# Softmax mixture on one core: VectorE makes the weights, and two stores are cut differently

## The chip, the cores and the metric

The kernel runs on one core of a Trainium2 chip. The metric is the device time of one execution in microseconds, as the median of the runs; lower is better. Five engines matter here: TensorE (PE, matmuls), VectorE (DVE), ScalarE (ACT), GpSimd (POOL) and SyncE (SP), which only issues transfers. Sixteen DMA engines move the data between HBM and the on-chip memory SBUF; TensorE writes its sums to PSUM. Each engine works through its own instructions in the order in which the program lists them, and waits on semaphores for the others.

## The reference

Four softmaxes over 4096 columns are mixed with weights that are themselves a softmax over the four heads:

```python
# logits: (32, 128, 4, 4096), prior: (32, 128, 4), float32
prior_probs = np.exp(prior - prior.max(axis=-1, keepdims=True))
prior_probs = prior_probs / prior_probs.sum(axis=-1, keepdims=True)
softmax = np.exp(logits - logits.max(axis=-1, keepdims=True))
softmax = softmax / softmax.sum(axis=-1, keepdims=True)
mixture = np.sum(prior_probs[..., None] * softmax, axis=2)   # (32, 128, 4096)
```

The input is 268 MB and the output 67 MB, and each is moved once.

## The kernel before

A unit is one of the 32 batches: 128 rows on the 128 partitions, four heads of 4096 columns. The tile `ring` has 12 slots of one head each, so three units lie in SBUF at a time. A head is worked on in place: it is loaded into its slot, its exponentials overwrite it, and the unit's result overwrites the slot of head 3 (`home`), from where it is stored.

The whole program is a list of words that `run` turns into instructions. A word is a letter for the step, the digits of its arguments (head, then first and last quarter of the columns), a prime for "the unit before", `+2` for "two units on" and `@u` for unit u. The steps are:

- `L` loads heads, `S` stores quarters of a unit (stores of units 2 to 21 are issued by ACT, all else by SP).
- `M` (VectorE) takes a row's negated maximum over 4096 columns, `E` (ACT) the exponentials with their row sum in `dsum`.
- `R` (VectorE) takes the reciprocal of that sum into `rden`. The weight of a head is this reciprocal times the prior probability `pp`.
- `G` (GpSimd) makes a 128x128 diagonal matrix of the weight: identity times `rden` times `pp`. `X` (TensorE) multiplies that diagonal with the exponentials and adds the heads up in PSUM (`acc`).
- `Z` (GpSimd) scales columns of a head by both numbers in place. `C` (GpSimd) multiplies both numbers into `wght`, which `K` (ACT, scaling) and `A`, `B`, `T` (VectorE, multiply by the weight and add) read.
- `O`, `P` and `W` (GpSimd) add columns of two slots, `V` (ACT) copies PSUM to SBUF.

So in a steady unit half of the columns go through TensorE for heads 0 to 2 and end with `A` on VectorE, and the other half are scaled by ACT (`K`) and GpSimd (`Z`) and added by GpSimd (`O`). The order of all this is written out by hand: `ORDER` has one line each for units 0 and 1, the line `STEADY` 22 times, and a long list for units 24 to 31 in which the steps of neighbouring units are interleaved. `BYPASS` names column quarters of which head 2 doesn't go through TensorE. Loads wait until the slots that they fill are free: for heads 0 to 2 until the last `O` of the old unit, for head 3 until its store has landed.

`store` cuts unit 28 (`U - 4`) into three transfers: the columns but the last 320 of all 128 rows, the last 320 of 125 rows, and the last 320 of the other 3 rows. Unit 31 is stored in halves, `S24` and `S02`.

Of the kernel before, what the change touches and what calls it, by code (L numbers as in the profile page):

```python
# [8 lines left out]
FP32 = mybir.dt.float32  # L9
AF = mybir.ActivationFunctionType  # L10
ALU = mybir.AluOpType
# [14 lines left out]

FIRST = "L02 L24"
STEADY = (
    "M0 E0 O224' R3' C3' Z324' M1 R0 G0 C0 O324' A01' A12' E1 S' L03+2 L34+2 K024 X002 "
    "M2 E2 R1 G1 X102 Z124 M3 E3 R2 G2 X202 C2 O124 K224 "  # L30
)

ORDER = [
# [3 lines left out]
] + [STEADY] * 22  # L37
ORDER += [
# [27 lines left out]
]  # L66

EXTRA = 320

BYPASS = {  # L70
    (27, 3), (28, 2), (28, 3), (29, 3), (30, 3), (31, 2), (31, 3),
# [4 lines left out]
def kernel(  # L76
# [6 lines left out]
    nc = tc.nc  # L83
    U, P, H, V = logits.shape
# [5 lines left out]
    C = V // 4  # L90

    cpool = ctx.enter_context(tc.tile_pool(name="cpool", bufs=1))
# [4 lines left out]

    nmax = cpool.tile([P, U, H], FP32, name="nmax")
    dsum = cpool.tile([P, U, H], FP32, name="dsum")
    rden = cpool.tile([P, U, H], FP32, name="rden")  # L100
    wght = cpool.tile([P, U, H], FP32, name="wght")
    diag = cpool.tile([P, 2, H - 1, P], FP32, name="diag")
    ident = cpool.tile([P, P], FP32, name="ident")
# [3 lines left out]
    pp = cpool.tile([P, H, U], FP32, name="pp")  # L107
# [4 lines left out]
    def slot(u, h, a=0, b=4):  # L112
        return ring[:, place(u, h), a * C : b * C]

    def home(u, a, b):
        return slot(u, 3, a, b)
# [8 lines left out]

    def store(u, a=0, b=4):
        queue = nc.scalar if 2 <= u < 22 else nc.sync
        if u == U - 4:

            o, c = home(u, a, b), V - EXTRA  # L130
            for p, q, i, j in ((0, P, 0, c), (0, 125, c, V), (125, P, c, V)):
                queue.dma_start(out=out[u, p:q, i:j], in_=o[p:q, i:j])
            return
        queue.dma_start(out=out[u, :, a * C : b * C], in_=home(u, a, b))

    def peak(u, h):
# [7 lines left out]
            accum_out=dsum[:, u, h : h + 1],  # L144
        )

    def recip(u, h):
        nc.vector.reciprocal(rden[:, u, h : h + 1], dsum[:, u, h : h + 1])  # L148

    def diagonal(u, h):  # L150
        nc.gpsimd.tensor_scalar(  # L151
            out=diag[:, u % 2, h], in0=ident, scalar1=rden[:, u, h : h + 1],
            scalar2=pp[:, h, u : u + 1], op0=ALU.mult, op1=ALU.mult,
        )


    def weigh(u, h, a=0, b=4):
        e = slot(u, h)
# [4 lines left out]
                start=h == 0, stop=h == H - 2 or (u, k * W // C) in BYPASS and h == H - 3,  # L163
            )

    def weight(u, h):
        nc.gpsimd.tensor_mul(wght[:, u, h : h + 1], rden[:, u, h : h + 1], pp[:, h, u : u + 1])  # L167

    def scale(u, h, a, b):
        e = slot(u, h, a, b)  # L170
        nc.gpsimd.tensor_scalar(  # L171
            out=e, in0=e, scalar1=rden[:, u, h : h + 1], scalar2=pp[:, h, u : u + 1],
            op0=ALU.mult, op1=ALU.mult,
        )

    def scale_act(u, h, a, b):
        e = slot(u, h, a, b)
# [28 lines left out]
    def add_scaled(u, a, b):  # L206
        nc.gpsimd.tensor_add(home(u, a, b), slot(u, 1, a, b), slot(u, 3, a, b))  # L207

    step = {
        "L": load, "S": store, "M": peak, "E": exp, "R": recip, "G": diagonal, "X": weigh,  # L210
        "C": weight, "Z": scale, "A": add_last, "B": add_head, "T": add_both, "V": evac,
        "P": add_scaled, "W": add_second,
        "K": scale_act, "O": add_below,
    }
# [10 lines left out]
    with tc.manual_schedule():  # L225
# [6 lines left out]
            out=ident, in_=ident, pattern=[[-1, P]], compare_op=ALU.is_equal, fill=0.0,  # L232
# [48 lines left out]
```

## Time and profile before

| | before |
|---|---|
| runs | 788.8, 786.51, 786.8 us; median 786.8 us |
| the profiled execution | 786.83 us, span 785.1 us |
| mean granted TensorE clock | 0.841 |
| busy: VectorE, ACT, GpSimd, TensorE | 82%, 75%, 73%, 60% of the span |
| moved by DMA | 335.83 MB, mean 428 GB/s |
| VectorE: 128 maxima of 4096 columns (line 137) | 563.0 us, 4409 ns each |
| ACT: 128 exponentials of 4096 columns (line 142) | 474.1 us, 3704 ns each |
| GpSimd: 68 additions of 2048 columns (line 182) | 308.5 us, 4537 ns each |
| GpSimd: 50 scalings of 2048 columns (line 171) | 102.4 us, 2047 ns each |
| GpSimd: 96 diagonals (line 151) | 43.0 us, 448 ns each |
| GpSimd: 79 weights of 128x1 (line 167) | 15.0 us, 189 ns each |
| VectorE: 128 reciprocals of 128x1 (line 148) | 19.4 us, 155 ns each |

The span runs from the first to the last instruction of the profiled execution; the time of the same execution is a little longer. Busy time is what an engine spent in instructions that compute. Times in the text are microseconds from the start of the span.

### The profile page before, as it was taken

The page shows a single profiled execution, that of the slowest core. Times are in us where ns is not written, and L with a number is a line of the kernel's source. Part 1 is how long each engine was busy: PE and PEld are TensorE (multiplying, and loading weights), DVE is VectorE, ACT ScalarE, POOL GpSimd, SP SyncE. Part 2 cuts the span into 40 slices and gives each one's busy share as a digit, 9 for nine tenths or more (in the row PEclk, how much of TensorE's full clock was granted, in tenths as well). Part 3 has the DMA queues.
Part 4 walks back from the last instruction along what each step waited for, and adds up shares of the span by engine and source line. Part 5 has one row for each costly group of instructions (what it writes and reads, how often), then busy time and mean ns, then how long its engine had stood idle before and what let it go on. Part 6 is the DMA issues. An engine that isn't in the chain of part 4 may idle for free.

```text
span 785.1 us, 3589 instructions
## 1 busy us (share of the span) xinstructions
PE 472.1 (60%) x920; PEld 189.7 (24%) x920; DVE 646.3 (82%) x326; ACT 590.1 (75%) x324; POOL 575.1 (73%) x342
## 2 busy tenths in 40 slices
PE   0445556554466444664446655456643988899996
PEld 0112212211122111221112222112211433334342
DVE  5589988797777977779877789777898877989895
ACT  1658887777878778787787877777878567779883
POOL 0799877788777788777887778877786434377892
PEclk9968898886887778887778777788777999999999
DMA  9999999999999999999999999999999999999997
GB/s 379 452 454 390 449 417 422 431 449 421 452 410 432 441 439 429 432 420 436 449 419 444 414 434 432 450 414 431 433 445 434 430 413 431 441 420 430 429 428 336
DMA packets 14747, 335.83 MB, mean 428 GB/s; under 512 B 1640, under 2 KB 1768, under 8 KB 1800
## 3 DMA queue, kind: packets, MB, share of 16 engines
q1 hardware_dynamic: 11800, 293.61, 87.1%
q10 hardware_dynamic: 2928, 42.01, 12.5%
q8 instruction: 7, 0.11, 0.1%
q14 instruction: 12, 0.10, 0.0%
HBM read 268.50 MB, written 67.11 MB: 427 GB/s over the span
## 4 chain that ended last, share of the span: by engine, by line
DMA 58%; DVE 21%; POOL 13%; issue 3%; PE 2%; ACT 2%; SPq 0%; POOLq 0%; ACTq 0%
DMA ring<-in_logits_dram 58%; DVE nmax L137 19%; POOL ring L182 9%; PE acc L160 2%; POOL ring L171 2%; POOL diag L151 1%; ACT ring L178 1%; DVE ring L185 1%; POOL ring L201 1%; POOL ring L207 1%; ACT ring L142 1%; DVE rden L148 0%; POOL wght L167 0%; ACT ring L204 0%; SPq L123 0%
## 5 line engine op out<-in xcount | busy, mean ns | idle before, releaser
L160 PE MATMUL acc<-ring,diag 128*128 128x512 f32 x920 | 472.1, 669 | 305.4 <-DVE ring L185 213.2
L137 DVE TENSOR_REDUCE nmax<-ring 128x1 f32<-128x4096 f32 x128 | 563.0, 4409 | 99.8 <-DMA ring<-in_logits_dram 99.8
L142 ACT ACTIVATE ring<-ring,nmax 128x4096 f32<-128x4096 f32 x128 | 474.1, 3704 | 122.7 <-DVE rden L148 72.8
L182 POOL TENSOR_TENSOR ring<-ring 128x2048 f32<-128x2048 f32 (+2 forms) x75 | 333.6, 4449 | 7.0 <-ACT ring L178 6.8
L160 PEld LDWEIGHTS acc<-ring,diag 128*128 128x128 f32 x920 | 189.7, 214 | 587.0 <-issue 212.3
L171 POOL TENSOR_SCALAR ring<-ring,rden,pp 128x2048 f32<-128x2048 f32 (+3 forms) x61 | 130.9, 2146 | 33.5 <-DVE rden L148 33.5
L151 POOL TENSOR_SCALAR diag<-ident,rden,pp 128x128 f32<-128x128 f32 x96 | 43.0, 448 | 133.5 <-DVE rden L148 129.0
L178 ACT ACTIVATE ring<-ring,wght 128x2048 f32<-128x2048 f32 x46 | 91.7, 1994 | 46.1 <-POOL ring L182 32.5
L185 DVE SCALAR_TENSOR_TENSOR ring<-ring,wght,acc 128x1024 f32<-128x1024 f32 x59 | 73.1, 1271 | 5.1 <-POOL wght L167 4.1
L207 POOL TENSOR_TENSOR ring<-ring 128x1024 f32<-128x1024 f32 x20 | 47.3, 2375 | 12.9 <-ACT ring L204 8.2
L148 DVE RECIPROCAL rden<-dsum 128x1 f32<-128x1 f32 x128 | 19.4, 155 | 19.3 <-ACT ring L142 19.2
L204 ACT ACTIVATE ring<-acc 128x1024 f32<-128x1024 f32 x20 | 20.0, 1012 | 6.3 <-issue 4.1
L142 ACT ACTIVATION_READ_ACCUMULATOR ring<-ring,nmax 128x1 f32 x128 | 23.9, 187 | 0.0
L167 POOL TENSOR_TENSOR wght<-rden,pp 128x1 f32<-128x1 f32 x79 | 15.0, 189 | 10.1 <-DVE rden L148 10.1
L201 POOL TENSOR_TENSOR ring<-ring 128x1024 f32<-128x1024 f32 x5 | 11.8, 2368 | 0.1
L236 DVE TENSOR_REDUCE pmax<-pr 32x128 f32<-32x512 f32 x1 | 0.7, 674 | 7.2 <-DMA pr<-in_prior_dram 7.2
L238 ACT ACTIVATE pr<-pr 32x512 f32<-32x512 f32 x1 | 0.6, 628 | 6.1 <-DVE pr L237 6.1
L185 DVE SCALAR_TENSOR_TENSOR ring<-ring,wght 128x1024 f32<-128x1024 f32 x2 | 2.5, 1282 | 0.3 <-POOL wght L167 0.3
L238 ACT ACT_TABLE_LOAD x1 | 1.3, 1283 | 1.2 <-PEq L265 1.2
L245 DVE STREAM_TRANSPOSE pp<-pn 32x128 f32<-32x128 f32 x4 | 1.2, 302 | 0.1
L239 DVE TENSOR_REDUCE pmax<-pr 32x128 f32<-32x512 f32 x1 | 0.7, 675 | 0.7 <-ACT pr L238 0.7
L241 DVE TENSOR_TENSOR pn<-pr,pmax 32x512 f32<-32x512 f32 x1 | 1.0, 1021 | 0.0
(8 smaller groups left out, 2.5 us busy)
## 6 DMA issues: line engine op xcount, KB each, us to landing
ring<-in_logits_dram SPq DMA_DIRECT2D x26, 6144.0 KB, 34.3
ring<-in_logits_dram SPq DMA_DIRECT2D x38, 2048.0 KB, 25.5
out_dram<-ring ACTq DMA_DIRECT2D x20, 2048.0 KB, 16.1
out_dram<-ring SPq DMA_DIRECT2D x10, 2048.0 KB, 14.0
ring<-in_logits_dram SPq DMA_DIRECT2D x2, 4096.0 KB, 12.5
out_dram<-ring SPq DMA_DIRECT2D x2, 1024.0 KB, 5.9
out_dram<-ring SPq DMA_DIRECT2D x1, 1888.0 KB, 33.8
out_dram<-ring SPq DMA_DIRECT2D x1, 156.2 KB
```

Of the source, the lines that this page charges most:

```text
L137: nc.vector.tensor_reduce(out=nmax[:, u, h : h + 1], in_=slot(u, h), op=ALU.max, axis=AX.X, negate=True)
L142: nc.scalar.activation(slot(u, h), slot(u, h), AF.Exp, bias=nmax[:, u, h : h + 1], accum_out=dsum[:, u, h : h + 1],)
L148: nc.vector.reciprocal(rden[:, u, h : h + 1], dsum[:, u, h : h + 1])
L151: nc.gpsimd.tensor_scalar(out=diag[:, u % 2, h], in0=ident, scalar1=rden[:, u, h : h + 1], scalar2=pp[:, h, u : u + 1], op0=ALU.mult, op1= ...
L160: nc.tensor.matmul(acc[:, k * W : (k + 1) * W], lhsT=diag[:, u % 2, h], rhs=e[:, k * W : (k + 1) * W], start=h == 0, stop=h == H - 2 or (u ...
L171: nc.gpsimd.tensor_scalar(out=e, in0=e, scalar1=rden[:, u, h : h + 1], scalar2=pp[:, h, u : u + 1], op0=ALU.mult, op1=ALU.mult,)
L178: nc.scalar.activation(e, e, AF.Copy, scale=wght[:, u, h : h + 1])
L182: nc.gpsimd.tensor_add(e, e, slot(u, h - 1, a, b))
L185: nc.vector.scalar_tensor_tensor(out=o, in0=slot(u, h, a, b), scalar=wght[:, u, h : h + 1], in1=more, op0=ALU.mult, op1=ALU.add,)
L201: nc.gpsimd.tensor_add(e, e, slot(u, 2, a, b))
L204: nc.scalar.activation(slot(u, 1, a, b), acc[:, a * C : b * C], AF.Copy)
L207: nc.gpsimd.tensor_add(home(u, a, b), slot(u, 1, a, b), slot(u, 3, a, b))
```

## The change

`R` becomes `weight`: on VectorE the reciprocal goes into `wght`, and a second VectorE instruction multiplies it in place by the prior. In a steady unit one `R02` does both for heads 0 and 1. The step `C` and the tile `rden` are gone. `Z` and `G` now take one scalar, the finished weight; `G02` builds two diagonals in one GpSimd instruction of two tensor inputs, the identity and the weight, both repeated by stride 0. In the steady line `R0 G0` move from behind `M1` to behind `M2`, as `R02` and `G02`; `K024` (ACT), which reads head 0's weight, stays behind the store, and `E1` and `O324'` come earlier; `A01' A12'` become one `A02'`. Unit 28 is stored in one transfer, and unit 31 in quarters instead of halves, in the order of columns 2, 3, 0, 1.

```diff
 STEADY = (
-    "M0 E0 O224' R3' C3' Z324' M1 R0 G0 C0 O324' A01' A12' E1 S' L03+2 L34+2 K024 X002 "
-    "M2 E2 R1 G1 X102 Z124 M3 E3 R2 G2 X202 C2 O124 K224 "
+    "M0 E0 O224' R3' Z324' M1 E1 O324' A02' S' L03+2 L34+2 M2 R02 K024 E2 G02 X002 "
+    "X102 Z124 M3 E3 R2 G2 X202 O124 K224 "
 )
...
-    "R3@31 C3@31 T23@31 X112@31 T34@31 X212@31 A01@31 S24@31 A12@31 S02@31 "
+    "R3@31 T23@31 X112@31 T34@31 X212@31 A01@31 S23@31 A12@31 S34@31 S01@31 S12@31 "
...
     def store(u, a=0, b=4):
         queue = nc.scalar if 2 <= u < 22 else nc.sync
-        if u == U - 4:
-
-            o, c = home(u, a, b), V - EXTRA
-            for p, q, i, j in ((0, P, 0, c), (0, 125, c, V), (125, P, c, V)):
-                queue.dma_start(out=out[u, p:q, i:j], in_=o[p:q, i:j])
-            return
         queue.dma_start(out=out[u, :, a * C : b * C], in_=home(u, a, b))
...
-    def recip(u, h):
-        nc.vector.reciprocal(rden[:, u, h : h + 1], dsum[:, u, h : h + 1])
-
-    def diagonal(u, h):
-        nc.gpsimd.tensor_scalar(
-            out=diag[:, u % 2, h], in0=ident, scalar1=rden[:, u, h : h + 1],
-            scalar2=pp[:, h, u : u + 1], op0=ALU.mult, op1=ALU.mult,
-        )
+    def weight(u, h, to=None):
+        k = to or h + 1
+        w = wght[:, u, h:k]
+        nc.vector.reciprocal(w, dsum[:, u, h:k])
+        nc.vector.tensor_mul(w, w, pp[:, h:k, u])
+
+    def diagonal(u, h, to=None):
+        if to is None:
+            nc.gpsimd.tensor_scalar_mul(diag[:, u % 2, h], ident, wght[:, u, h : h + 1])
+            return
+        s = [P, to - h, P]
+        nc.gpsimd.tensor_mul(
+            diag[:, u % 2, h:to], ident.unsqueeze(1).to_broadcast(s),
+            wght[:, u, h:to].unsqueeze(2).to_broadcast(s),
+        )
...
-    def weight(u, h):
-        nc.gpsimd.tensor_mul(wght[:, u, h : h + 1], rden[:, u, h : h + 1], pp[:, h, u : u + 1])
-
     def scale(u, h, a, b):
         e = slot(u, h, a, b)
-        nc.gpsimd.tensor_scalar(
-            out=e, in0=e, scalar1=rden[:, u, h : h + 1], scalar2=pp[:, h, u : u + 1],
-            op0=ALU.mult, op1=ALU.mult,
-        )
+        nc.gpsimd.tensor_scalar_mul(e, e, wght[:, u, h : h + 1])
```

In units 24 to 31 the words `C` are left out and nothing else of their order changes, up to the stores of unit 31.

More of the change, by code (lines that the diff above doesn't have):

```diff
@@ L61 @@
     "P23@29 X101@30 L23@31 V34@30 R2@30 R3@30 G2@30 M1@31 E0@31 Z314@30 X223@30 X201@30 "
[1 row of a table removed]
[1 row of a table added]
     "X001@31 P34@30 S@28 V12@30 X034@31 P23@30 R1@31 E2@31 M3@31 X012@31 G1@31 P12@30 "
[2 rows of a table removed]
[2 rows of a table added]
 ]
-EXTRA = 320
 BYPASS = {
@@ L99 @@
     dsum = cpool.tile([P, U, H], FP32, name="dsum")
-    rden = cpool.tile([P, U, H], FP32, name="rden")
     wght = cpool.tile([P, U, H], FP32, name="wght")
@@ L209 @@
     step = {
-        "L": load, "S": store, "M": peak, "E": exp, "R": recip, "G": diagonal, "X": weigh,
-        "C": weight, "Z": scale, "A": add_last, "B": add_head, "T": add_both, "V": evac,
+        "L": load, "S": store, "M": peak, "E": exp, "R": weight, "G": diagonal, "X": weigh,
+        "Z": scale, "A": add_last, "B": add_head, "T": add_both, "V": evac,
         "P": add_scaled, "W": add_second,
```

22 rows, old and new, of the table ORDER are left out of this document.

## The prediction

> **What bounds the kernel now.** I read the page first: its slices, then the DMA queues.
>
> ```profile
> span 785.1 us, 3589 instructions
> DMA  9999999999999999999999999999999999999997
> q1 hardware_dynamic: 11800, 293.61, 87.1%
> q10 hardware_dynamic: 2928, 42.01, 12.5%
> ```
>
> The two queues' packets fill 99.6% of sixteen DMA engines' time. No compute engine is above 82%. The second view is the busy time by windows (the last two columns are DMA share and GB/s):
>
> ```profile
> 20.00:770.00 750.00, 464.57 (x903) 186.68 (x904) 627.34 (x310) 583.44 (x321) 574.27 (x335) 0.84 1.00 431
> 770.00:785.20 15.20, 7.52 (x18) 3.04 (x16) 7.08 (x7) 2.47 (x2) 0.19 (x1) 0.88 0.74 310
> ```
>
> Up to 770 the share is 1.00, and only the last 15 us have holes. So a compute edit costs nothing until it lets the transfers run dry, or until the end. The third view is the DMA view from 782.2 to 785.2 (forty slices of GB/s):
>
> ```profile
> GB/s 109 110 219 0 109 109 218 0 109 0 109 0 0 0 109 0 0 0 0 109 0 0 0 0 0 0 0 0 0 0 0 0 0 0 0 0 0 0 0 0
> DMA packets 28, 0.10 MB, mean 33 GB/s; under 512 B 16, under 2 KB 16, under 8 KB 16
> ```
>
> Sixteen of the 28 are semaphore writes, twelve are 8 KB pieces of the last store, and the last ones go out singly, one slice in four or five: one DMA engine finishes alone. In the trace's packet records each packet starts 3 to 4 ns before the previous one of its engine ends, so engines can be followed. Most end their last data at 782.3, three at 782.9 to 783.1, one at 783.94, and that one has no gap after the start. The span ends 1.17 after it (785.1), and the execution's 786.83 is 1.73 more than the span; the runs' median is 786.8. The kernel is bound by the work of its slowest DMA engine.
>
> The fourth view is the timeline of a steady iteration (a unit takes 24.23 us, from one store's issue, 317.39, to the next, 341.62):
>
> ```profile
> 303.21 4.42 DVE L137 TENSOR_REDUCE nmax<-ring 128x1 f32<-128x4096 f32 x1 [3.76 <-DMA ring<-in_logits_dram]
> 312.26 0.45 POOL L151 TENSOR_SCALAR diag<-ident,rden,pp 128x128 f32<-128x128 f32 x1 [0.58 <-DVE rden L148]
> 317.39 0.36 ACTq L134 DMA_DIRECT2D out_dram<-ring  x1
> ```
>
> VectorE waits 3.76 us for a load, and the load issued beside that store lands 34.3 us later, of which its 6.3 MB need 14.5 at 433 GB/s and the store beside it 4.9: about 15 us of queue stand ahead of it.
>
> **The store of unit 28 (the term that moves the time).** Now it is three pieces. In the packet records the 320 columns of 125 rows lie on five engines, 25 packets of 1280 B each, and the other eleven get none. A full 16 KB packet takes 0.611 us, a 15 KB one 0.561, a 1280 B one 0.052. Five engines spend 8 x 0.561 + 25 x 0.052 = 5.79, eleven 4.49; in one transfer each spends 8 x 0.611 = 4.89. So five engines gain 0.90 and eleven lose 0.40. The slowest engine is one of the five: it starts its 15 KB packets at 763.52, the small ones at 768.01, and the next store at 769.31. Gain: 0.90 us. With it the five are the four latest engines before the small packets; the latest of the eleven starts the next store at 766.6, 1.4 before where the slowest will then be (768.4), so losing 0.40 there hides. Its end goes from 783.94 to 783.04.
> The Trainium skill (DMA: Bandwidth & Descriptors, "Why a DMA increments its semaphore by 16 and not by 1") says that such a transfer takes the largest k up to 16 that divides the row count, on the lowest-numbered engines. The trace agrees with the five, and by that rule they are the same five in every execution.
>
> SP issues this store once instead of three times, saving two issues of 0.4 and a 4.0 us wait; behind them stands only unit 29's store, held by GpSimd until 753.07. Worth nothing.
>
> **Unit 31 in quarters.** 32 packets of 4 KB for 16 of 8 KB: from 0.611 (16 KB) and 0.3065 (8 KB) about 2 ns of overhead each, so +0.04, and two semaphore packets of 9 ns: +0.05 us. The last quarter needs 1.24 us on an engine, not 2.47. Today the last add ends at 778.84, SP issues at 778.87, the first packet is at 779.70. The slowest engine will reach the last quarter at 781.9, so the final adds may be 1.9 us later at no cost. Two more SP issues of 0.33 fall in pauses between the adds.
>
> **The weights.** Removed: 79 GpSimd multiplies (189 ns). Added: a VectorE multiply behind each reciprocal (once for heads 0 and 1 in a steady unit). The trace has no VectorE multiply of 128x1; the nearest row is the reciprocal, 155 ns, of which 70 show when the next instruction isn't dependent. Bounds 0.07 to 0.35, taken 0.2 for the multiply with its dependence. VectorE per steady unit: 4 x 4.41 + 2.46 + 3 x 0.35 = 21.2 of 24.23. GpSimd: three multiplies (0.5) go, two diagonals (0.42 each) become one two-input instruction of 256 columns: from 2375 ns for 1024 and 4537 for 2048, 0.21 + 256 x 2.11 ns = 0.75. Less work by 0.6. Scaling by one scalar instead of two I leave at the 2.05 us of now (bounds 1.9, ACT's for the same form, and 2.2).
> The new wait: K024 on ACT needs R02, which stands behind M2 on VectorE; queued behind K024 are E2, E3, K224, and behind these O224. From the load's landing: M0 4.4, R3 0.35, M1 4.4, A02 2.46, M2 4.4, R02 0.35: K024 starts at 16.4, where it now starts at 14.6. E2 then ends at 22.3 and R2 at 22.7, before the next landing at 24.23: 1.5 us to spare. GpSimd, no longer holding O324 behind G0, ends it at 14.7 against 14.2: load and store are issued 0.5 later under 15 us of queue. Nothing.
> At the start there is less cover: the three loaded units last to 60.66 and the first store is issued at 58.91. An issue takes 0.86 to its first packet (769.25 to 770.11), so it may come at 59.8. R3 and R0 add 0.4 ahead of G0, C0's 0.15 goes: 59.2. Covered.
> In the tail (units 24 to 31) four multiplies a unit are 0.8 us against some 4 us of VectorE idle; loads have over 20 us of queue. After the last wait for a load (754.24) three multiplies (0.6) delay the final adds, and 0.71 and 0.31 of waiting for GpSimd's weights go: even.
>
> Sum: 785.1 - 0.90 + 0.05 = 784.25 span, + 1.73 = **786.0 us**. 0.3% (2.4 us) is about what a measurement of this kernel can tell from no change, and this is less.
>
> **Rivals.**
> *VectorE's multiply waits for GpSimd (slower).* It is the kernel's first VectorE instruction with two SBUF inputs beside a working GpSimd: the adds on VectorE take one input from PSUM, and the two that don't (772.97) run with GpSimd idle. So the trace leaves open whether it must wait for the GpSimd instruction in progress, 0 to 4.5 us. The place that decides is the end:
>
> ```profile
> 761.78 4.69 POOL L207 TENSOR_TENSOR ring<-ring 128x1024 f32<-128x1024 f32 x2
> 764.16 0.15 DVE L148 RECIPROCAL rden<-dsum 128x1 f32<-128x1 f32 x1
> 777.56 1.28 DVE L185 SCALAR_TENSOR_TENSOR ring<-ring,wght,acc 128x1024 f32<-128x1024 f32 x1 [0.92 <-PE acc L160]
> ```
>
> At 764.16 (unit 31, head 1) 2.2 us of the add are left, at 743.90 1.6 were; unit 31's M3 starts behind them. Followed row by row (M1 1.7 late, M2 2.2, M3 4.3; then E3, R3, four adds) the last add ends at 782.4; + 0.86 + 1.24 + 1.17 = 785.7 span. At the start the reciprocals at 46.67 and 56.64 meet adds with 0.8 and 2.1 left, and the first store slips to 60.1: 0.3 us of idle DMA. 787.4 to 787.8. In steady units the waits only shift what 15 us of queue cover, for when R2 leads the next M0 the gap between O124 and O224 lets the multiply in. It decides once the final adds are over 1.9 us late. Against: most reciprocals (25 of the 33 after 600) end while GpSimd is idle, waiting for that weight.
> The Trainium skill (SBUF — State Buffer, "Who interferes with whom") says that a VectorE instruction with two SBUF inputs and a GpSimd instruction that reads SBUF block one another fully, for the whole instruction. By that rule this rival holds; no run here shows it.
>
> *The slow engine is another one.* Instruction fetches (the page's queues 8 and 14: 7 and 12 packets) fall on single engines; if one of the eleven is last, 0.40 is lost, not 0.90 won: 787.2. Against: four of the five were late in the profiled execution.
>
> *The steady unit outgrows the transfers.* If the loop K024, E2, R2, M0, R3, M1, A02, M2, R02 (22.7 with all in place) passes 24.23, all 22 units pay and 15 us of queue pay the first part: at 26 us, 22 x 1.8 - 15 = 25 us, 812. It needs 1.5 us of new waits per unit, lasting.
>
> *The rest of the slowest engine's lag goes too (faster).* The next latest engine starts its 15 KB packets at 762.66, 0.9 before the slowest: were that gone as well (another spread of the fetches), the end would be 785.1. Over 0.3% faster (784.4) needs faster packets: no engine's sum in this trace allows it.
>
> **How the numbers follow.** Forecast, with the smaller lag in it, 0.46; waiting multiply 0.32, a quarter of it with knock-on waits past 789.2; other engine 0.12; steady unit 0.07; faster than any sum 0.03. Range: down to the second engine's 785.1 less the 0.3 by which a run of before lies under the profiled execution, 784.8, up to 789.0, which takes in the rival's 787.8 and the 788.8 among the runs before; 0.15 lies above, 0.03 below. Faster 0.03, slower 0.08 + 0.07 = 0.15, same 0.82.
>
> **What would show it.** In the profile after: no 1280 B packets, DMA share 1.00 to 770, last data at about 783.0 and one engine still alone; VectorE's multiply at 0.1 to 0.2 us (rival: 1 us or more in the mean, or M rows starting late behind it). K024 starting 16.4 after the landing, VectorE's wait for the load still there (gone: third rival). Wrong if DMA shows a hole before 770, or if the last store's issue is past 781.

## The result: 878.1 us after 787.1, and the profile after

| | before | after |
|---|---|---|
| median of the runs | 787.12 us (786.51 to 788.8) | 878.06 us (877.82 to 880.5) |
| ratio | | 1.116 (95% interval 1.1148 to 1.1172) |
| span of the profiled execution | 785.1 us | 876.2 us |

The change costs 91 us, and the prediction (786.0, range 784.8 to 789.0) is wrong. The page of after, in the parts that were shown of before, and three groups of instructions (count, then busy us and mean ns of one, then idle time before them, with what ended it):

```profile
span 876.2 us, 3509 instructions
DMA  9974998999999989999999999899999999999944
q1 hardware_dynamic: 11952, 293.61, 81.2%
q10 hardware_dynamic: 2928, 42.01, 11.2%
L165 POOL TENSOR_SCALAR ring<-ring,wght 128x2048 f32<-128x2048 f32 (+3 forms) x61 | 349.9, 5737 | 25.6 <-DVE wght L142 21.9
L173 POOL TENSOR_TENSOR ring<-ring 128x2048 f32<-128x2048 f32 (+2 forms) x75 | 333.3, 4445 | 3.8
L142 DVE TENSOR_TENSOR wght<-wght,pp 128x1 f32<-128x1 f32 (+1 forms) x106 | 132.4, 1249 | 3.6
```

The first two of these groups in the page of before:

```profile
L171 POOL TENSOR_SCALAR ring<-ring,rden,pp 128x2048 f32<-128x2048 f32 (+3 forms) x61 | 130.9, 2146 | 33.5 <-DVE rden L148 33.5
L182 POOL TENSOR_TENSOR ring<-ring 128x2048 f32<-128x2048 f32 (+2 forms) x75 | 333.6, 4449 | 7.0 <-ACT ring L178 6.8
```

The DMA queues fill 92.4% of the sixteen engines' time where they filled 99.6%. GpSimd's additions (L173) are as they were, but its 61 scalings take 349.9 us where they took 130.9: 219 us more, at the same number and size. VectorE's new multiply (84 of one column, 22 of two) has a mean of 1249 ns. The windows (DMA share and GB/s in the last two columns):

```profile
60.00:78.00 18.00, 5.52 (x9) 2.30 (x10) 16.78 (x8) 13.06 (x8) 18.00 (x8) 0.63 0.00 0
20.00:770.00 750.00, 392.76 (x752) 163.20 (x752) 669.75 (x324) 515.59 (x280) 693.77 (x198) 0.76 0.94 390
770.00:876.20 106.20, 79.49 (x169) 33.70 (x168) 90.80 (x55) 68.25 (x43) 90.07 (x38) 0.90 0.79 334
```

The share of 1.00 up to 770 is gone, and from 60 to 78 the transfers stand still while GpSimd (the fifth busy column) is busy for all 18 us. At the very end (873.3 to 876.3) one DMA engine still finishes alone, but with these holes the transfers no longer set the time:

```profile
GB/s 382 492 328 437 382 492 382 219 0 0 55 0 0 0 55 0 0 0 55 0 0 0 0 0 0 0 0 0 0 0 0 0 0 0 0 0 0 0 0 0
DMA packets 75, 0.25 MB, mean 82 GB/s; under 512 B 16, under 2 KB 16, under 8 KB 74
```

A steady unit in the timeline:

```profile
303.94 5.45 POOL L165 TENSOR_SCALAR ring<-ring,wght 128x2048 f32<-128x2048 f32 x1
305.88 4.41 DVE L128 TENSOR_REDUCE nmax<-ring 128x1 f32<-128x4096 f32 x1
309.48 4.49 POOL L173 TENSOR_TENSOR ring<-ring 128x2048 f32<-128x2048 f32 x1
310.39 3.60 DVE L142 TENSOR_TENSOR wght<-wght,pp 128x2 f32<-128x2 f32 x1
314.00 0.36 ACTq L125 DMA_DIRECT2D out_dram<-ring  x1
314.13 0.61 POOL L149 TENSOR_TENSOR diag<-ident,wght 128x256 f32<-128x256 f32 x1 [0.16 <-DVE wght L142]
314.72 5.44 POOL L165 TENSOR_SCALAR ring<-ring,wght 128x2048 f32<-128x2048 f32 x1
320.72 0.60 POOL L146 TENSOR_SCALAR diag<-ident,wght 128x128 f32<-128x128 f32 x1 [0.56 <-PE acc L157]
321.29 9.18 POOL L173 TENSOR_TENSOR ring<-ring 128x2048 f32<-128x2048 f32 x2
330.43 5.45 POOL L165 TENSOR_SCALAR ring<-ring,wght 128x2048 f32<-128x2048 f32 x1
```

From one scaling to the same one a unit later, 303.94 to 330.43, are 26.49 us, and GpSimd has next to no pause in them: three additions (13.6), two scalings (10.9) and the diagonals' two instructions (1.2) are 25.7. The transfers would need 24.23. VectorE's wait for a load ahead of a maximum (3.76 us before) is gone.

The 91.1 us of span by stretches: the first store is issued at 77.18 instead of 58.91 (18.3 more; four scalings of 3072 columns ahead of it take 8.0 each instead of 2.9), from there to unit 22's store are 581.2 instead of 525.1 (56.1 more), and from there to the end 217.8 instead of 201.1 (16.7 more).

Two suspects are left by these lines, and both are in the same units. Theory F (for form) is the scaling by one scalar. Theory W (for wait) is VectorE's multiply that waits for GpSimd; above, the multiply of 310.39 ends at 313.99, with the addition of 309.48 to 313.97.

### The profile page after: what moved, and what is told of

It reads as the page before. It is cut to its first block, busy times and chain, and to the rows that moved or that the text cites. A ratio compares the mean times of both kernels' runs of the same rounds, so it can differ in the third digit from the quotient of the medians.

```text
span 876.2 us, 3509 instructions
## 1 busy us (share of the span) xinstructions
PE 472.3 (54%) x920; PEld 196.9 (22%) x920; DVE 772.6 (88%) x388; ACT 588.1 (67%) x324; POOL 784.5 (90%) x241
## 4 chain that ended last, share of the span: by engine, by line
POOL 53%; DVE 13%; ACT 10%; issue 9%; DMA 8%; PE 6%; ACTq 1%; POOLq 0%; SPq 0%
POOL ring L173 33%; POOL ring L165 17%; DVE nmax L128 9%; ACT ring L133 9%; DMA ring<-in_logits_dram 8%; PE acc L157 6%; DVE wght L142 2%; POOL diag L146 2%; DVE ring L176 1%; ACTq L125 1%; DVE wght L141 1%; POOL ring L198 1%; ACT ring L169 0%; ACT ring L195 0%; SPq L120 0%
## 5 line engine op out<-in xcount | busy, mean ns | idle before, releaser
L165 POOL TENSOR_SCALAR ring<-ring,wght 128x2048 f32<-128x2048 f32 (+3 forms) x61 | 349.9, 5737 | 25.6 <-DVE wght L142 21.9
L157 PEld LDWEIGHTS acc<-ring,diag 128*128 128x128 f32 x920 | 196.9, 219 | 672.7 <-POOL diag L149 318.7
L173 POOL TENSOR_TENSOR ring<-ring 128x2048 f32<-128x2048 f32 (+2 forms) x75 | 333.3, 4445 | 3.8
L142 DVE TENSOR_TENSOR wght<-wght,pp 128x1 f32<-128x1 f32 (+1 forms) x106 | 132.4, 1249 | 3.6
L176 DVE SCALAR_TENSOR_TENSOR ring<-ring,wght,acc 128x2048 f32<-128x2048 f32 (+1 forms) x37 | 70.4, 1903 | 27.6 <-PE acc L157 27.6
L141 DVE RECIPROCAL wght<-dsum 128x1 f32<-128x1 f32 (+1 forms) x106 | 16.3, 154 | 51.4 <-ACT ring L133 51.4
L146 POOL TENSOR_SCALAR diag<-ident,wght 128x128 f32<-128x128 f32 x52 | 31.3, 602 | 33.0 <-DVE wght L142 21.7
L133 ACT ACTIVATION_READ_ACCUMULATOR ring<-ring,nmax 128x1 f32 x128 | 23.9, 187 | 0.0
L149 POOL TENSOR_TENSOR diag<-ident,wght 128x256 f32<-128x256 f32 x22 | 13.5, 612 | 3.5 <-DVE wght L142 3.5
```

The costliest lines, as they stand in the source:

```text
L133: nc.scalar.activation(slot(u, h), slot(u, h), AF.Exp, bias=nmax[:, u, h : h + 1], accum_out=dsum[:, u, h : h + 1],)
L141: nc.vector.reciprocal(w, dsum[:, u, h:k])
L142: nc.vector.tensor_mul(w, w, pp[:, h:k, u])
L146: nc.gpsimd.tensor_scalar_mul(diag[:, u % 2, h], ident, wght[:, u, h : h + 1])
L157: nc.tensor.matmul(acc[:, k * W : (k + 1) * W], lhsT=diag[:, u % 2, h], rhs=e[:, k * W : (k + 1) * W], start=h == 0, stop=h == H - 2 or (u ...
L165: nc.gpsimd.tensor_scalar_mul(e, e, wght[:, u, h : h + 1])
```

## The experiments

Each ratio is against times of the kernel before from the same chip. Their median is 787.52 for the first four experiments, 787.06 for `a_imm`, `b_28`, `b_31` and `a_three`, and 786.77 for the other four.

**Each suspect alone, both, and the form in the kernel before.**

`a_two`, GpSimd's two-scalar form back:

```diff
-        nc.gpsimd.tensor_scalar_mul(e, e, wght[:, u, h : h + 1])
+        nc.gpsimd.tensor_scalar(out=e, in0=e, scalar1=wght[:, u, h : h + 1], scalar2=one,
+                                op0=ALU.mult, op1=ALU.mult)
```

Here `one` is a column of 1.0; the single diagonals are changed in the same way.

> The changed kernel with GpSimd's scalings and single diagonals in the two-scalar form of before (second scalar a column of ones); VectorE's multiplies stay. Theory F (the one-scalar form is slow: 5.44 us where the two-scalar form took 2.05): GpSimd's steady unit falls from 26.4 us by 2 x 3.39 to about 19.5, under the transfers' 24.23, so 786 to 792. Theory W (VectorE's multiply, which waits for GpSimd, is what costs): the waits of 116 us on VectorE stay, and with them at least 40 of the 91 us: 830 or more.

Measured: 788.98 us, ratio 1.0017 (1.0007 to 1.0026). The groups of this run:

```profile
L169 POOL TENSOR_SCALAR ring<-ring,wght,one 128x2048 f32<-128x2048 f32 x50 | 102.4, 2048 | 6.7 <-issue 4.1 <-DVE wght L143 1.8
L143 DVE TENSOR_TENSOR wght<-wght,pp 128x1 f32<-128x1 f32 x84 | 58.4, 696 | 2.9
L143 DVE TENSOR_TENSOR wght<-wght,pp 128x2 f32<-128x2 f32 x22 | 6.6, 301 | 0.8
```

One more multiplication per element, and a scaling of 2048 columns takes 2048 ns instead of 5440. With that alone 89 of the 91 us are back, as theory F has it. VectorE's single multiplies still wait (696 ns in the mean, 711 in the kernel after), but those of two weights fell from 3301 to 301 ns, so this run alone took away a part of the wait too. The next one takes the wait away and leaves the form.

`a_ptr`, the multiply with one tensor input, the prior read as a scalar per partition:

```diff
-        nc.vector.tensor_mul(w, w, pp[:, h:k, u])
+        for j in range(h, k):
+            nc.vector.tensor_scalar(out=wght[:, u, j : j + 1], in0=wght[:, u, j : j + 1],
+                                    scalar1=pp[:, j, u : u + 1], scalar2=None, op0=ALU.mult)
```

> The changed kernel with VectorE's multiply by a scalar read per partition (one tensor input instead of two, R02 as two multiplies); GpSimd's one-scalar form stays. F: GpSimd stays the bound at 25.5 to 26.4 us a unit, 860 to 878. W: the multiplies fall from 1.25 us mean to under 0.2 and the time to 785 to 800.

Measured: 875.63 us, ratio 1.1116 (1.1099 to 1.1133). The multiply fell to 212 ns in the mean (202 to 216), so the wait is gone, and the time stayed:

```profile
L143 DVE TENSOR_SCALAR wght<-wght,pp 128x1 f32<-128x1 f32 x128 | 25.3, 212 | 3.8
L169 POOL TENSOR_SCALAR ring<-ring,wght 128x2048 f32<-128x2048 f32 x50 | 271.9, 5438 | 2.9 <-issue 2.9
```

VectorE spends 107 us less in these multiplies (132.4 before this edit), and the time falls by 2.4 of the 91 us (by 3.5, taken from the two ratios). So the wait isn't the cause.

`a_both`, both edits.

> Both edits together: two-scalar form on GpSimd, one-tensor multiply on VectorE. F and W alike: transfers bind again, 785 to 788; by the prediction's first term, 0.8 under before. If it stays over 800, the order or the stores cost what neither theory has.

Measured: 786.96 us, ratio 0.9994 (0.9985 to 1.0004). The transfers bind again, and VectorE waits for a load as before:

```profile
304.76 4.42 DVE L129 TENSOR_REDUCE nmax<-ring 128x1 f32<-128x4096 f32 x1 [2.03 <-DMA ring<-in_logits_dram]
```

So the order and the stores don't explain the 91 us; what is left of them, 1 to 2 us, is in the runs of the stores below. Against `a_two`, on the same chip, the wait is worth 2.0 us.

`b_one`, the form alone, in the kernel before:

```diff
-        nc.gpsimd.tensor_scalar(out=e, in0=e, scalar1=rden[:, u, h : h + 1],
-                                scalar2=pp[:, h, u : u + 1], op0=ALU.mult, op1=ALU.mult)
+        nc.gpsimd.tensor_scalar_mul(e, e, rden[:, u, h : h + 1])
```

> The kernel before with GpSimd's scaling by the reciprocal alone in the one-scalar form (it leaves out the prior's factor in the scaled columns). F: each scaling of 2048 columns takes 5.4 instead of 2.05, GpSimd's unit goes to some 26 us and the time to 840 to 880. W: no VectorE multiply is there, so 787.

Measured: 885.16 us, ratio 1.1236 (1.1214 to 1.1259), a little over the 840 to 880 expected. There is no other edit in it, so the slow form alone does what the change did. It takes 7 us more than the change; in its trace a steady unit is 27.03 us (307.60 to 334.63) instead of 26.49, and GpSimd has three weights of 0.19 us in it that the change had removed.

```profile
L171 POOL TENSOR_SCALAR ring<-ring,rden 128x2048 f32<-128x2048 f32 x50 | 271.6, 5431 | 4.2 <-DVE rden L148 4.2
```

**What makes the form slow.** `a_imm` is `a_two` with `scalar2=1.0` in place of the column.

> As the run with a column of ones, but the second scalar is the constant 1.0 in the instruction. If the number of operations decides, a scaling of 2048 columns takes 2.05 us as with two scalar columns, and the time is 789; if it must be two scalar columns, it stays at 5.4 us and 870.

Measured: 788.17 us, ratio 1.0017 (1.0007 to 1.0027).

```profile
L168 POOL TENSOR_SCALAR ring<-ring,wght 128x2048 f32<-128x2048 f32 x50 | 98.6, 1972 | 7.8 <-issue 5.3 <-DVE wght L142 1.8
```

It reads the same single column `wght` as the slow one, and is the fastest of the three. So it isn't the number of scalar columns read; it is whether the instruction has a second operation. Why GpSimd runs the one-operation form slower isn't shown by these runs.

**A half dose.** `a_half` is `a_both` with the one-scalar form for head 1 in units 2 to 23, one of the two scalings of a unit.

> The repaired kernel with the one-scalar form for head 1's scaling alone, in units 2 to 23 (one of two scalings a unit). GpSimd's unit goes from 19.4 to 22.8 us, still under the transfers' 24.23, so if the cost comes only when GpSimd's unit outgrows the transfers: 787 to 788. If each slow scaling costs its 3.4 us or a part of it wherever it stands: 22 x 3.4 = 75 us at most, 37 at half, 825 or more.

Measured: 788.14 us, ratio 1.0012 (1.0003 to 1.0021).

```profile
L174 POOL TENSOR_SCALAR ring<-ring,wght 128x2048 f32<-128x2048 f32 x22 | 119.6, 5437 | 0.0
L176 POOL TENSOR_SCALAR ring<-ring,wght,one 128x2048 f32<-128x2048 f32 x28 | 57.5, 2052 | 8.8 <-issue 6.8 <-DVE wght L144 2.0
```

22 slow scalings add 22 x 3.385 = 74.5 us to GpSimd, and the time stays within 1.5 us of `a_both`'s. This fits a cost that comes only when GpSimd's unit passes that of the transfers, 24.23: by its rows (three additions, the scalings, the diagonals) one slow scaling leaves it at 22.2 us, two bring it to 25.7 and, with its pauses, 26.5. These two doses are all that was measured.

**The wait by itself.** `b_mul` puts a multiply that nobody reads into the kernel before:

```diff
         nc.vector.reciprocal(rden[:, u, h : h + 1], dsum[:, u, h : h + 1])
+        nc.vector.tensor_mul(spare[:, u, h : h + 1], dsum[:, u, h : h + 1], pp[:, h, u : u + 1])
```

> The kernel before with one VectorE multiply of 128x1 of two SBUF inputs (row sum times prior, into a tile that nothing reads) behind each reciprocal. Theory W: where GpSimd is in an addition or scaling the multiply lasts until that ends, so some rows of 1 to 4 us beside many of 0.16, and 0 to 3 us on the time, from the last units. Without such a wait: all rows 0.16, and 787.

Measured: 788.9 us, ratio 1.0022 (1.0013 to 1.0031).

```profile
L150 DVE TENSOR_TENSOR spare<-dsum,pp 128x1 f32<-128x1 f32 x128 | 69.9, 547 | 0.0
755.63 0.13 DVE L150 TENSOR_TENSOR spare<-dsum,pp 128x1 f32<-128x1 f32 x1
766.08 2.02 DVE L150 TENSOR_TENSOR spare<-dsum,pp 128x1 f32<-128x1 f32 x1
```

The same instruction takes 0.13 us or, with GpSimd in an addition, 2.02. The time is 2.1 us longer, and the place fits the last units, as theory W had it: the last store is issued at 781.67 instead of 778.87, while the transfers' share up to 770 is 1.00 as before.

**The stores.** `b_28` and `b_31` are the kernel before with one of the two store edits of the change, `b_2831` with both; `a_three` is `a_both` with unit 28 in three pieces as before.

> The kernel before with unit 28 stored in one transfer, nothing else. The prediction's first term: 0.9 us faster, for the slowest engine is one of the five that carry the 1280 B packets. Rival (another engine is the slow one): 0.4 slower.

Measured: 786.46 us, ratio 0.9992 (0.9983 to 1.0001): 0.6 us less, not quite clear of no change.

> The kernel before with unit 31 stored in quarters, nothing else. The prediction: the slowest engine has the same bytes, +0.05 us, not to be told from no change. Rival (the last store's arrival sets the end): 1.2 us faster.

Measured: 787.1 us, ratio 1.0002 (0.9993 to 1.0011): nothing, as forecast.

> The repaired kernel (two-scalar form, one-tensor multiply) with unit 28 in three pieces as before. If the pieces cost 0.9 us, 787.9 against the 787.0 of one transfer; if they relieve the slow engine, 786.6.

Measured: 788.93 us, ratio 1.0022 (1.0012 to 1.0032). `a_both` stood at 0.9994 (0.9985 to 1.0004), each against its own runs of before: the pieces cost 0.28%, some 2.2 us, in the repaired kernel, more than expected. Why they cost more there than in the kernel before isn't shown. The run shows one thing more: with the stores of before for unit 28, the new order and weights (with unit 31 in quarters, worth nothing alone) are 0.22% slower than the kernel before.

> The kernel before with unit 28 in one transfer and unit 31 in quarters, the weights left on GpSimd: 0.6 under before from the first (measured alone), 0 from the second; 786.3 to 786.6.

Measured: 786.09 us, ratio 0.9988 (0.9979 to 0.9997). This is the one version whose interval lies wholly under 1, by 0.1%: the stores of the change without its weights. Its profiled execution has a span of 784.3 us, where the prediction's sum had 784.25.

**The change with both causes out, in the cheapest form** (`a_immptr`: the constant 1.0 on GpSimd, the one-tensor multiply on VectorE).

> The changed kernel with both causes taken out in the cheapest form: GpSimd scales by the weight and the constant 1.0 (1.97 us for 2048 columns), VectorE multiplies by a scalar read per partition. 786.5 to 787: level with before, transfers bind.

Measured: 787.47 us, ratio 1.0003 (0.9995 to 1.0012): level with before. Moving the weights to VectorE, done without its two costs, gains nothing, for the transfers bind. Against `b_2831`, which has the same stores and the same times of before, it is 1.4 us slower: what the stores win, the new order and weights lose. Which wait that is isn't shown.

## Why the prediction was wrong, step by step

- **The step that failed** is one sentence of the part on the weights: "Scaling by one scalar instead of two I leave at the 2.05 us of now (bounds 1.9 ... and 2.2)". It measured 5.44 us, and with two such scalings a unit GpSimd, not the transfers, set the time. The trace of before has no GpSimd instruction of that form; its nearest row was another form, and the upper bound was drawn just over that row without a reason. GpSimd's own additions, 4.54 us for the same size, stood in the same table as a far higher bound. Three additions and two scalings at 4.54 and the two diagonal instructions at 1.2 together are 23.9 us a unit, right under the transfers' 24.23, and the risk would have been seen. Even that bound was too low: the measured scaling is slower than the addition, and only a run of the form could give its price.
- **What bounds the kernel** was right for the kernel before, and the cover was real: the half dose hides 74.5 us of GpSimd's work. But the cover was checked for VectorE's and ACT's loop alone. GpSimd's sum per unit was written only as a saving ("less work by 0.6"), not held against 24.23 with its bounds. The sign that the prediction set for this, a hole in the DMA share before 770, is there (60 to 78).
- **The rival "the steady unit outgrows the transfers"**, at 0.07, is the kind of case that came. Its loop (VectorE and ACT) was the wrong one, and its price formula gives, at 26.49, 22 x 2.26 - 15 = 34.7 us where 56.1 came between the first store and unit 22's, with 18.3 at the start and 16.7 at the end beside it. Nothing of the 15 us of queue shows in the 56.1: these 22 units take 26.42 us each (581.2 / 22) where they took 23.87. The start was costed for VectorE's 0.4 us, not for four scalings of 3072 columns.
- **The rival "VectorE's multiply waits for GpSimd"** holds, at its place: in `a_two` the multiply of unit 31's head 1 lasts 2.12 us, where 2.2 of an addition were to be left. The sign set for it, a mean of 1 us or more, came too (1249 ns in the kernel after), and still the wait is only 2.4 (by the ratios 3.5) of the 91 us.

```profile
767.29 0.15 DVE L142 RECIPROCAL wght<-dsum 128x1 f32<-128x1 f32 x1
767.48 2.12 DVE L143 TENSOR_TENSOR wght<-wght,pp 128x1 f32<-128x1 f32 x1
769.51 4.41 DVE L129 TENSOR_REDUCE nmax<-ring 128x1 f32<-128x4096 f32 x1
```

  The Trainium skill (SBUF — State Buffer, "Who interferes with whom") has the engine that comes second wait for the other's whole instruction; beside GpSimd's additions and two-operation scalings the traces agree, with 0.16 us for a free multiply and up to 5.7 for one that meets GpSimd at work (`a_two`). Beside a one-operation scaling the wait is shorter than that (the last section). The rival priced `a_two`'s case at 787.4 to 787.8; it measured 788.98.
- **Right in size:** a multiply that needn't wait (0.2 forecast with its dependence; in the kernel after reciprocal and multiply take 0.28 up to the next maximum, 320.19 to 320.47, where the reciprocal alone took 0.07), unit 31 in quarters (+0.05; no change measured), K024's new place (16.4 us after VectorE starts on the load; 16.1 in `a_both`: 304.76 to 320.83). The double diagonal is 0.61 where 0.75 stood.
- **The store of unit 28** was forecast at -0.90 us. Alone it measured -0.6 with an interval that just takes in zero, and with the quarters (`b_2831`) the gain is clear of zero, -0.7 by the medians. In the repaired kernel the same cut is worth 2.2. The sign is shown, the size only roughly.

## What to carry to other kernels

Write down each engine's sum per iteration against the bound's, with the upper bound of every changed instruction in it, not only the difference; here one engine had 5 us of room and two instructions could each take 2.5 of it. An instruction that looks like a shorter form of a measured one is another instruction: until it has a row of its own, its bounds are far-off rows, also above, and here the price lay beyond even those. And while the transfers bind, as here, an edit on an engine with slack can at best gain nothing, so its bad cases deserve the working.

## What the runs showed of the hardware that was not expected

- GpSimd's scaling by a scalar per partition takes 2854, 5438, 8040 and 10630 ns for 1024, 2048, 3072 and 4096 columns with one operation (`a_ptr`), and 1203, 2053, 2908 and 3761 ns with two (`a_both`): 2.53 against 0.83 ns per further column. A second operation that does nothing (times 1.0) makes it 2.65 times as fast at 2048 columns; with the constant in the instruction it is 1972 ns. The 128x128 diagonals show the same: 602 against 448 ns, and 372 with the constant.
- VectorE's multiply of two SBUF inputs of one column, 0.16 us, waits for GpSimd's instruction, also when nobody needs its result (`b_mul`); the same product with one tensor input and a scalar read per partition takes 0.21 us whatever GpSimd does (202 to 216 ns in `a_ptr`).
- How long it waits depends on GpSimd's instruction. In the kernel after, all 41 multiplies that meet an addition of 2048 columns end with it, within 0.03 us. The nine that wait for a one-operation scaling, of 2048, 3072 or 4096 columns, end 1.71 to 1.72 us before the scaling does. Ten that start in its last 1.54 us take 0.16 us and don't wait at all. The few that meet a two-operation scaling (`a_two`, `a_imm`, `b_mul`) end with it, within 0.01 us. In the kernel after:

```profile
92.76 5.43 POOL L165 TENSOR_SCALAR ring<-ring,wght 128x2048 f32<-128x2048 f32 x1
95.95 0.53 DVE L142 TENSOR_TENSOR wght<-wght,pp 128x2 f32<-128x2 f32 x1
```

  The scaling ends at 98.19, the multiply at 96.48. Why the wait ends early there isn't shown.
